# Sums of feed-forward weight quarters: by accumulating loads, or by GpSimd

## The chip, the cores and the metric

The kernel runs on one core of a Trainium2 chip. The metric is the device time of one execution in microseconds (us). Engines are called as the profile calls them: PE (TensorE, matrix products; PEld is its weight load), DVE (VectorE), ACT (ScalarE), POOL (GpSimd), SP (the queue that issues most loads).

## The reference

A small encoder of two layers, 512 tokens of width 1024, everything in 32-bit floats. Each layer is a feed-forward block, a token mixer (attention), attention into 256 memory tokens, and a second feed-forward block, each followed by a layer norm. So there are four feed-forward blocks. This is the part that matters here, with `D_FF` = 2816:

```python
def swiglu(x, w_gate, w_up, w_down):
    return (jax.nn.silu(x @ w_gate) * (x @ w_up)) @ w_down
...
        y = swiglu(x, ffn_w_gate[i, 0], ffn_w_up[i, 0], ffn_w_down[i, 0])
        x = layer_norm(ALPHA * x + 0.5 * y, ln_g[i, 0], ln_b[i, 0])
```

## The kernel before

**Precision.** Every product is made of three reduced-precision products (`mm3`): an operand is split into a high part, a cast by ACT, and a low part, the residue `source - high` by DVE (`split`, and `wide` for a weight tile of 128x1024). All operands of a product must be split before PE can begin it.

**Seven products for eight.** Inside a feed-forward block, most of the work is done in groups of 512 hidden columns (two ranges of 256, `c1` and `c2`) by a scheme of the Strassen-Winograd kind: a 2 x 2 block product with seven block products, named 1 to 7, in place of eight, at the price of sums of quarters of the operands. `quarters` does this for gate and for up. Its four weight quarters are called here a = (0, c1), c = (0, c2), d = (1, c2), b = (1, c1), where 0 and 1 are the halves of the 1024 input rows. Product 1 uses a, 2 uses b, 4 uses d, 5 uses c + d, 7 uses a + c, 6 uses a + c + d, 3 uses a + b + c + d. `down_steps` does it for the down weights, with quarters 11, 12, 22, 21: t1 = 12 + 11 (product 5), t2 = t1 + 22 (product 6), t3 = 12 + 22 (product 7), and t2 + 21 (product 4).

**How the sums are made before.** Two sums of gate and up (c + d and a + c) and two of down (t1 and t3) are made by DMA: SP loads the first quarter into a tile, and then POOL issues a load of the second quarter into the same tile that adds (`accum_op=ALU.add`). So some quarters are loaded more than once. The other sums (two each) are made by DVE (`mix`).

**Tiles.** Weight quarters, their split parts and hidden activations all live in 27 buffers of 128x1024 floats (tag `slab`), given out in program order. A load can start when its buffer is free. Products go into PSUM banks: three with tag `a` (hidden products), two `d`, three `t`.

**Order.** Every product is a step with three parts, `load`, `prep` (sums and splits) and `product`; `pipeline` calls load three steps and prep one step ahead of the product, and the steps of group g's hidden products alternate with those of the down products of group g - 1. There are four groups after the first in each block (16 in all), and a tail: 256 columns without the scheme, and the last down group, whose results POOL gathers with 128x512 sums into `x` (`gather`). But the instructions aren't issued as they are called: `Graph.record` keeps them, and `Graph.emit` schedules them by a list scheduler with costs in ns from `Graph.cost` and the dependencies of the tiles. Every instruction therefore has line 143 in the profile (`op.call`), and is told by its tiles. Names ending in numbers are single tiles; the profile leaves the numbers out, so the working tiles `t2` and the PSUM banks `t` both read `t` there.

Of the kernel before, what the change touches and what calls it, by code (L numbers as in the profile page):

```python
# [12 lines left out]
F32 = mybir.dt.float32  # L13
# [4 lines left out]
ALU = mybir.AluOpType  # L18
AX = mybir.AxisListType

P = 128
# [42 lines left out]
class Graph:  # L64
# [44 lines left out]
    @staticmethod  # L109
    def cost(engine, method, out, ins, kw):  # L110
        n = 1
        for d in (out if method != "tensor_reduce" else ins[0]).ap[1:]:
            n *= d[1]
        wide = any(z.space == bass.MemoryType.PSUM for z in ins + [out]) if engine != "sync" else False
        if method == "dma_start":
            return max(n * out.ap[0][1] * 4 / 205.0, 600.0) if engine == "sync" else 700.0
        if engine == "tensor":
            return max(n / 2.4 + 14, 111)
        scalars = sum(1 for z in ins if z.ap[-1][1] == 1)
        if engine == "vector":  # L120
            if method == "tensor_scalar" and not wide:
                n = n / 2
            return n / 0.96 + 72 + 60 * scalars + 120 * (method == "scalar_tensor_tensor" and "accum_out" in kw)
        if engine == "scalar":
            return n / 1.2 + (55 if wide else 100) + 45 * scalars + 130 * ("accum_out" in kw)
        if n <= 8:
            return 270.0 if method == "tensor_scalar" else 500.0
        adds = len(ins) == 1 and ins[0].ap[-1][0] != 0 and n == 512
        return n * (0.83 if method == "memset" else 4.2 if adds else 1.85) + 60

    def record(self, engine, method, args, kw):
        kw = dict(kw)
# [120 lines left out]
class Kernel:  # L253
# [276 lines left out]
            ps = self.transposed([(t * P, P, sgs[t][:, b * P : (b + 1) * P]) for t in range(NT)])  # L530
            self.nc.scalar.copy(dst[:, :, b, :], ps.rearrange("p (s n) -> p s n", s=2))

    def load_sum(self, *parts):

        z = self.slab(F32, (P, 4, 256))
        for i, (w, q, c) in enumerate(parts):
            src = w[512 * q : 512 * q + 512, c : c + 256].rearrange("(k p) f -> p k f", p=P)
            if i == 0:
                self.nc.sync.dma_start(out=z, in_=src)
            else:  # L540
                self.nc.gpsimd.dma_start(out=z, in_=src, accum_op=ALU.add)
        return z

    def wide(self, z):
# [1 line left out]
        self.split(z, *got)  # L546
        return got

    def mix(self, dst, x, y, op):
        self.nc.vector.tensor_tensor(out=dst, in0=x, in1=y, op=op)  # L550
        return dst

    def w_halves(self, w, c0):
        return [self.wide(self.load_sum((w, q, c0))) for q in range(2)]

    def hidden(self, wg, wu, c0, dst=None):

# [35 lines left out]
    def quarters(self, w, c1, c2, xs, h, gate, up):  # L593


        nc, mix = self.nc, self.mix
        flat = lambda z: z.rearrange("p b n -> p (b n)")
        raw, left, own = {}, {}, {}
        parts = {
            1: [(w, 0, c1)], 6: [(w, 0, c2), (w, 1, c2)], 2: [(w, 1, c1)], 7: [(w, 0, c1), (w, 0, c2)], 4: [(w, 1, c2)],  # L600
        }
        fill, onto = (1, 6, 5), {2: 1, 7: 6, 4: 6, 3: 5}

        def load(m):
            if m in parts:
                raw[m] = self.load_sum(*parts[m])

        def prep(m):
            if m == 6:
                z = mix(raw[1], raw[6], raw[1], ALU.add)  # L610
            elif m == 3:
                z = mix(raw[2], raw[1], raw[2], ALU.add)
            else:
                z = raw[6 if m == 5 else m]
            left[m] = self.wide(z)

        def done(f, s, z):
            if up:
                if not h:
                    h.extend(self.slab(F32, (P, 2, 2, 256)) for _ in range(2))  # L620
                mix(flat(h[f][:, s]), z, gate[f, s], ALU.mult)
            else:
                y = self.t2(F32) if s == 0 else z
                nc.scalar.activation(y, z, AF.Silu)
                gate[f, s] = y

        def product(m):
            if m in fill:
                own[m] = self.ps("a")
            ps, wt = own[onto.get(m, m)], left.pop(m)  # L630
            for b in range(2):
                for k in range(4):
                    self.mm3(
                        ps[:, b * 256 : b * 256 + 256], [z[:, k, b * P : (b + 1) * P] for z in wt],
                        [z[:, k, :] for z in xs[m]], m in fill and b == 0 and k == 0, k == 3, skip_group_check=True,
                    )
            if m == 1:
                own["c12"], own["c22"] = self.t2(F32), self.t2(F32)
                nc.scalar.copy(own["c12"], ps)
            elif m == 6:  # L640
                mix(ps, ps, own["c12"], ALU.subtract)
                nc.scalar.copy(own["c12"], ps)
            elif m == 5:
                nc.scalar.copy(own["c22"], ps)
            elif m == 7:
                mix(own["c22"], ps, own["c22"], ALU.subtract)
                done(1, 1, own["c22"])
            elif m == 3:
                mix(own["c12"], ps, own["c12"], ALU.subtract)
# [12 lines left out]
    def down_steps(self, h, w, r1, r2, coef, u2, last, fresh=False):  # L662


        nc, mix = self.nc, self.mix
        quarters = {"11": (r1, 0), "12": (r1, 512), "22": (r2, 512), "21": (r2, 0)}
        part = lambda name: w[quarters[name][0] : quarters[name][0] + 256, quarters[name][1] : quarters[name][1] + 512]
        raw, left, right, banks, sums = {}, {}, {}, {}, {}
        flat = lambda z: z.rearrange("p b n -> p (b n)")
        act = lambda i, j: flat(h[j - 1][:, i - 1])  # L670

        def fetch(name, plus=None):

            z = self.slab(F32, (P, 2, 512))
            nc.sync.dma_start(out=z, in_=part(name).rearrange("(b p) f -> p b f", p=P))
            if plus:
                nc.gpsimd.dma_start(out=z, in_=part(plus).rearrange("(b p) f -> p b f", p=P), accum_op=ALU.add)
            return z

        def load(m):  # L680
            if m == 1:
                raw["11"] = fetch("11")
            elif m == 6:
                raw["t1"], raw["22"] = fetch("12", "11"), fetch("22")
            elif m == 2:
                raw["21"] = fetch("21")
            elif m == 7:
                raw["t3"] = fetch("12", "22")

        def prep(m):  # L690
            if m == 6:
                raw["t2"] = mix(self.slab(F32, (P, 2, 512)), raw["t1"], raw["22"], ALU.add)
                sums[1] = mix(self.t2(F32), act(2, 2), act(2, 1), ALU.subtract)
                sums[2] = mix(self.t2(F32), sums[1], act(1, 1), ALU.add)
            elif m == 4:
                mix(raw["21"], raw["t2"], raw["21"], ALU.add)
            elif m == 3:
                sums[4] = mix(self.t2(F32), sums[2], act(1, 2), ALU.subtract)
            elif m == 7:
                sums[3] = mix(self.t2(F32), act(1, 1), act(2, 1), ALU.subtract)  # L700
            right[m] = self.wide(raw[{1: "11", 6: "t2", 2: "21", 5: "t1", 3: "22", 7: "t3", 4: "21"}[m]])
# [57 lines left out]
    def ffn(self, i, ln_i, last, aside=None):  # L759

        nc = self.nc
# [32 lines left out]
        tail, wt, ln, ws = [], {}, {}, []  # L794
        for b in range(2):
            for name, w in (("gate", wg), ("up", wu)):

                def load(name=name, w=w):
                    wt[name] = [self.load_sum((w, q, 2560)) for q in range(2)]
# [12 lines left out]

                steps.append((load if b == 0 else none, prep if b == 0 else none, product))
# [717 lines left out]
```

## Time and profile before

| | |
|---|---|
| median of 3 runs | 2249.34 us (2249.16 to 2257.21) |
| the profiled execution | 2246.8 us, of which the span is 2245.0 us |
| granted clock of PE, mean | 0.985 |
| busy: PE, DVE, ACT, POOL | 96%, 75%, 47%, 18% of the span |
| HBM read, written | 301.06 MB, 4.19 MB |

The page gives the busy time of each engine, in all and in 40 slices, the DMA queues, the costliest groups of instructions with what ended the idle time before them, and the DMA issues. q1 in it holds the loads issued by SP, q0 those issued by POOL. A row of a group reads: line, engine, operation, output<-inputs, shape, count | busy us, mean ns of one | idle us before, with the releaser. A row of the timeline reads: start in us from the span's start, length in us, engine, operation, tiles, count of merged instructions, and in brackets the idle time before it and what ended it.

### The profile page before, as it was taken

To read this page: it belongs to the slowest core of one execution; us is meant where nothing else is said; L and a number is where in the kernel's file an instruction comes from. 1 tells how busy PE (TensorE), PEld (TensorE's weight loads), DVE (VectorE), ACT (ScalarE), POOL (GpSimd) and SP (SyncE) were. 2 spreads that over 40 slices of the span, in tenths; PEclk is the share of its full clock that TensorE was granted. 3 is DMA by queue.
4 is the path that set the end of the run, shared out by engine and by line. 5 is a ranking of instruction groups with operands and counts; after the bars stand their busy time and mean duration, and the time that the engine had idled before them with its cause. 6 is when DMAs were issued, how large, how long until landed. Compare 5 with 4: busy or idle time off the path is not lost. (4 is left out here: it accounts for less than half of the span.)

```text
span 2245.0 us, 34046 instructions
## 1 busy us (share of the span) xinstructions
PE 2158.3 (96%) x13408; PEld 1936.2 (86%) x13408; DVE 1689.0 (75%) x2429; ACT 1064.1 (47%) x1671; POOL 398.1 (18%) x499
## 2 busy tenths in 40 slices
PE   9989998999999999999999999999999999999998
PEld 7979887778898898988789998788989989998886
DVE  7678877788854867977767888876677458687886
ACT  5554443467443544544435554435554435454442
POOL 0111004644100001110211111314330000110102
PEclk9999999999999999999999999999999999999999
DMA  7777662201442348776446777535653324577662
GB/s 225 168 165 189 163 176 76 72 10 49 131 142 93 106 126 222 176 176 181 121 102 165 174 174 178 178 96 140 167 159 118 127 86 121 133 183 173 174 174 75
DMA packets 249808, 317.95 MB, mean 142 GB/s; under 512 B 11824, under 2 KB 193712, under 8 KB 249648
## 3 DMA queue, kind: packets, MB, share of 16 engines
q1 hardware_dynamic: 201040, 248.40, 35.7%
q0 software_dynamic: 48320, 67.12, 17.3%
q8 instruction: 105, 1.72, 0.3%
q14 instruction: 55, 0.45, 0.1%
q10 hardware_dynamic: 288, 0.26, 0.0%
HBM read 301.06 MB, written 4.19 MB: 136 GB/s over the span
## 5 line engine op out<-in xcount | busy, mean ns | idle before, releaser
L143 DVE TENSOR_TENSOR slab<-slab,slab 128x1024 fp32r<-128x1024 f32 (+3 forms) x582 | 660.9, 1160 | 159.0 <-ACT slab L143 87.5
L143 ACT CAST slab<-slab 128x1024 fp32r<-128x1024 f32 (+2 forms) x478 | 455.2, 984 | 317.9 <-DMA slab<-ffn_w_gate 93.8
L143 PE MATMUL a<-slab,slab 128*128 128x256 f32 (+3 forms) x2744 | 595.3, 309 | 2.3 <-DVE slab L143 1.2
L143 PE MATMUL a<-xh,slab 128*128 128x256 f32 (+2 forms) x2480 | 559.8, 315 | 1.2 <-ACT slab L143 1.2
L143 PEld LDWEIGHTS a<-slab,slab 128*128 128x128 f32 x2744 | 452.9, 193 | 34.5 <-DVE slab L143 5.0
L143 PE MATMUL d<-slab,slab 128*128 128x512 f32 (+2 forms) x1856 | 456.2, 384 | 5.9 <-ACT slab L143 3.1
L143 PEld LDWEIGHTS a<-xh,slab 128*128 128x128 f32 x2480 | 417.0, 191 | 34.7 <-ACT slab L143 2.1
L143 PE MATMUL a<-raw,slab 128*128 128x256 f32 x2048 | 402.9, 289 | 38.0 <-DVE t L143 31.7
L143 PE MATMUL a<-xl,slab 128*128 128x256 f32 (+1 forms) x1240 | 390.5, 315 | 0.0
L143 PEld LDWEIGHTS d<-slab,slab 128*128 128x128 f32 x1856 | 330.4, 190 | 63.2 <-ACT slab L143 4.8
L143 PEld LDWEIGHTS a<-raw,slab 128*128 128x128 f32 x2048 | 337.1, 197 | 51.5 <-DVE t L143 39.1
L143 PEld LDWEIGHTS a<-xl,slab 128*128 128x128 f32 x1240 | 236.4, 191 | 17.8
L143 PE MATMUL t<-slab,slab 128*128 128x512 f32 (+1 forms) x792 | 195.3, 386 | 7.7 <-ACT slab L143 4.6
L143 DVE TENSOR_TENSOR slab<-raw,slab 128x1024 fp32r<-128x1024 f32 (+2 forms) x140 | 170.6, 1236 | 13.3 <-ACT slab L143 12.9
L143 PEld LDWEIGHTS t<-slab,slab 128*128 128x128 f32 x792 | 138.6, 191 | 33.2 <-ACT slab L143 5.0
L143 ACT CAST slab<-t 128x512 fp32r<-128x512 f32 (+2 forms) x205 | 109.8, 564 | 120.3 <-PE t L143 66.8
L143 DVE TENSOR_TENSOR slab<-t,slab 128x512 fp32r<-128x512 f32 (+2 forms) x205 | 129.8, 656 | 28.6 <-ACT slab L143 28.4
L143 POOL TENSOR_TENSOR t<-t,l 128x256 f32<-128x256 f32 (+2 forms) x104 | 84.4, 832 | 369.1 <-DVE l L143 368.8
L143 ACT CAST slab<-raw 128x1024 fp32r<-128x1024 f32 (+1 forms) x132 | 131.4, 1026 | 22.9 <-DMA raw<-mem_w_kv 7.9
L143 DVE SCALAR_TENSOR_TENSOR x<-d,x 128x512 f32<-128x512 f32 x164 | 111.5, 685 | 29.4 <-PE d L143 28.8
L143 ACT COPY t<-a 128x512 f32<-128x512 f32 x96 | 56.0, 584 | 155.8 <-PE a L143 81.6
L143 POOL DMA_DIRECT2D slab<-ffn_w_up x32 | 41.0, 1282 | 437.4 <-DVE slab L143 176.9
(124 smaller groups left out, 2273.6 us busy)
## 6 DMA issues: line engine op xcount, KB each, us to landing
slab<-ffn_w_gate SPq DMA_DIRECT2D x102, 512.0 KB
slab<-ffn_w_up SPq DMA_DIRECT2D x102, 512.0 KB
slab<-ffn_w_down SPq DMA_DIRECT2D x100, 512.0 KB
slab<-ffn_w_down POOLq DMA_DIRECT2D x40, 512.0 KB, 8.0
slab<-ffn_w_gate POOLq DMA_DIRECT2D x32, 512.0 KB, 7.7
slab<-ffn_w_up POOLq DMA_DIRECT2D x32, 512.0 KB, 6.3
slab<-t SPq DMA_DIRECT2D x96, 128.0 KB
raw<-mem_w_kv SPq DMA_DIRECT2D x8, 1024.0 KB
```

The source lines that it names most:

```text
L143: op.call = lambda: fn(*args, **kw)
```

## The change

Each quarter is loaded once, by SP, into a tile of its own (`quarter` in place of `load_sum`, and `fetch` without `plus`). The sums that the accumulating loads made are made by POOL: v = a + c into a new tile and c += d in place for gate and up, t1 = 12 + 11 into a new tile and 12 += 22 in place for down (`mix` with `aside`). DVE makes the same number of sums as before: a += c after POOL's c += d (which gives a + c + d), a += b, t2 = t1 + 22, t2 += 21. Load m = 6 now takes c and v, load m = 5 takes d. In the scheduler's costs a POOL sum of 1024 columns is now put at 3.8 ns a column.

```diff
-        adds = len(ins) == 1 and ins[0].ap[-1][0] != 0 and n == 512
-        return n * (0.83 if method == "memset" else 4.2 if adds else 1.85) + 60
+        adds = n == 1024 or len(ins) == 1 and ins[0].ap[-1][0] != 0 and n == 512
+        return n * (0.83 if method == "memset" else 3.8 if adds else 1.85) + 60
...
-    def mix(self, dst, x, y, op):
-        self.nc.vector.tensor_tensor(out=dst, in0=x, in1=y, op=op)
+    def mix(self, dst, x, y, op, aside=False):
+        (self.nc.gpsimd if aside else self.nc.vector).tensor_tensor(out=dst, in0=x, in1=y, op=op)
         return dst
...
-        parts = {
-            1: [(w, 0, c1)], 6: [(w, 0, c2), (w, 1, c2)], 2: [(w, 1, c1)], 7: [(w, 0, c1), (w, 0, c2)], 4: [(w, 1, c2)],
-        }
+        places = {1: ("a", 0, c1), 6: ("c", 0, c2), 5: ("d", 1, c2), 2: ("b", 1, c1)}
...
         def load(m):
-            if m in parts:
-                raw[m] = self.load_sum(*parts[m])
+            if m in places:
+                name, q, c = places[m]
+                raw[name] = self.quarter(w, q, c)
+            if m == 6:
+                raw["v"] = mix(self.slab(F32, (P, 4, 256)), raw["a"], raw["c"], ALU.add, True)
+            elif m == 5:
+                mix(raw["c"], raw["c"], raw["d"], ALU.add, True)
 
         def prep(m):
             if m == 6:
-                z = mix(raw[1], raw[6], raw[1], ALU.add)
+                mix(raw["a"], raw["a"], raw["c"], ALU.add)
             elif m == 3:
-                z = mix(raw[2], raw[1], raw[2], ALU.add)
-            else:
-                z = raw[6 if m == 5 else m]
-            left[m] = self.wide(z)
+                mix(raw["a"], raw["a"], raw["b"], ALU.add)
+            left[m] = self.wide(raw[{1: "a", 6: "a", 5: "c", 2: "b", 7: "v", 4: "d", 3: "a"}[m]])
...
             elif m == 6:
-                raw["t1"], raw["22"] = fetch("12", "11"), fetch("22")
+                fetch("12")
+                fetch("22")
+                raw["t1"] = mix(self.slab(F32, (P, 2, 512)), raw["12"], raw["11"], ALU.add, True)
             elif m == 2:
-                raw["21"] = fetch("21")
-            elif m == 7:
-                raw["t3"] = fetch("12", "22")
+                fetch("21")
+                mix(raw["12"], raw["12"], raw["22"], ALU.add, True)
...
-            elif m == 4:
-                mix(raw["21"], raw["t2"], raw["21"], ALU.add)
+            elif m == 2:
+                mix(raw["t2"], raw["t2"], raw["21"], ALU.add)
```


On POOL, in the first feed-forward block, where the third and fourth groups' weights are handled, before (a DMA is an accumulating load, with the tile it adds into):

```order
L143 DMA slab_318_399<-ffn_w_down 128x2x512
L143 DMA slab_338_419<-ffn_w_gate 128x4x256
L143 DMA slab_355_436<-ffn_w_down 128x2x512
L143 DMA slab_358_439<-ffn_w_gate 128x4x256
L143 DMA slab_384_465<-ffn_w_up 128x4x256
L143 DMA slab_406_487<-ffn_w_up 128x4x256
```

And in the change (slab_334 is a, slab_338 is c, slab_343 is d and slab_339 is v of a gate; slab_357, 340 and 358 are 12, 11 and 22 of a down group):

```order
L143 TENSOR_TENSOR slab_339_420<-slab_334_415,slab_338_419 128x1024
L143 TENSOR_TENSOR slab_338_419<-slab_338_419,slab_343_424 128x1024
L143 TENSOR_TENSOR slab_359_440<-slab_357_438,slab_340_421 128x1024
L143 TENSOR_TENSOR slab_357_438<-slab_357_438,slab_358_439 128x1024
L143 TENSOR_TENSOR slab_386_467<-slab_382_463,slab_385_466 128x1024
L143 TENSOR_TENSOR slab_385_466<-slab_385_466,slab_395_476 128x1024
```

Each accumulating load has become one sum on POOL, and the two sums of one weight now stand next to each other. The same gate on DVE before, where slab_334 is a and slab_338 is the sum of c and d by DMA (TENSOR_SCALAR with a bank d or t empties a down product):

```order
L143 TENSOR_SCALAR x3_7_88<-d_333_414,x3_7_88 128x512
L143 TENSOR_TENSOR slab_334_415<-slab_338_419,slab_334_415 128x1024
L143 TENSOR_TENSOR slab_353_434<-slab_338_419,slab_352_433 128x1024
L143 TENSOR_TENSOR t2_300_381<-a_314_395,t2_300_381 128x512
L143 TENSOR_TENSOR slab_343_424<-slab_334_415,slab_342_423 128x1024
```

And in the change, where DVE's sum into slab_334 and the residue of slab_338 come after POOL's second sum:

```order
L143 TENSOR_TENSOR t2_302_383<-a_317_398,t2_302_383 128x512
L143 TENSOR_TENSOR slab_320_401<-t2_302_383,t2_256_337 128x512
L143 TENSOR_SCALAR x2_6_87<-d_330_411,x2_6_87 128x512
L143 TENSOR_TENSOR slab_334_415<-slab_334_415,slab_338_419 128x1024
L143 TENSOR_SCALAR x3_7_88<-d_333_414,x3_7_88 128x512
L143 TENSOR_TENSOR slab_345_426<-slab_334_415,slab_344_425 128x1024
L143 TENSOR_TENSOR slab_355_436<-slab_338_419,slab_354_435 128x1024
```

DVE's sum has moved behind one more down product, and the sum that empties a bank "a" into t2 is now ahead of it; the instructions are the same in kind and number.

More of the change, by code (lines that the diff above doesn't have):

```diff
@@ L531, in ffn_by_tokens, with quarter @@
             self.nc.scalar.copy(dst[:, :, b, :], ps.rearrange("p (s n) -> p s n", s=2))
-    def load_sum(self, *parts):
+    def quarter(self, w, q, c):
         z = self.slab(F32, (P, 4, 256))
[L536 to L539, printed above, removed]
-            else:
-                self.nc.gpsimd.dma_start(out=z, in_=src, accum_op=ALU.add)
+        self.nc.sync.dma_start(out=z, in_=w[512 * q : 512 * q + 512, c : c + 256].rearrange("(k p) f -> p k f", p=P))
         return z
@@ L547, in wide @@
         return got
-    def mix(self, dst, x, y, op):
-        self.nc.vector.tensor_tensor(out=dst, in0=x, in1=y, op=op)
+    def mix(self, dst, x, y, op, aside=False):
+        (self.nc.gpsimd if aside else self.nc.vector).tensor_tensor(out=dst, in0=x, in1=y, op=op)
         return dst
     def w_halves(self, w, c0):
-        return [self.wide(self.load_sum((w, q, c0))) for q in range(2)]
+        return [self.wide(self.quarter(w, q, c0)) for q in range(2)]
     def hidden(self, wg, wu, c0, dst=None):
@@ L598, in quarters @@
         raw, left, own = {}, {}, {}
-        parts = {
-            1: [(w, 0, c1)], 6: [(w, 0, c2), (w, 1, c2)], 2: [(w, 1, c1)], 7: [(w, 0, c1), (w, 0, c2)], 4: [(w, 1, c2)],
-        }
         fill, onto = (1, 6, 5), {2: 1, 7: 6, 4: 6, 3: 5}
+        places = {1: ("a", 0, c1), 6: ("c", 0, c2), 5: ("d", 1, c2), 2: ("b", 1, c1)}
         def load(m):
-            if m in parts:
-                raw[m] = self.load_sum(*parts[m])
+            if m in places:
[5 more added lines that the diff above has]
+                mix(raw["c"], raw["c"], raw["d"], ALU.add, True)
         def prep(m):
             if m == 6:
-                z = mix(raw[1], raw[6], raw[1], ALU.add)
+                mix(raw["a"], raw["a"], raw["c"], ALU.add)
             elif m == 3:
-                z = mix(raw[2], raw[1], raw[2], ALU.add)
-            else:
-                z = raw[6 if m == 5 else m]
-            left[m] = self.wide(z)
+                mix(raw["a"], raw["a"], raw["b"], ALU.add)
+            left[m] = self.wide(raw[{1: "a", 6: "a", 5: "c", 2: "b", 7: "v", 4: "d", 3: "a"}[m]])
         def done(f, s, z):
@@ L670, in down_steps, with fetch @@
         act = lambda i, j: flat(h[j - 1][:, i - 1])
-        def fetch(name, plus=None):
-            z = self.slab(F32, (P, 2, 512))
+        def fetch(name):
+            z = raw[name] = self.slab(F32, (P, 2, 512))
             nc.sync.dma_start(out=z, in_=part(name).rearrange("(b p) f -> p b f", p=P))
-            if plus:
-                nc.gpsimd.dma_start(out=z, in_=part(plus).rearrange("(b p) f -> p b f", p=P), accum_op=ALU.add)
-            return z
         def load(m):
             if m == 1:
-                raw["11"] = fetch("11")
+                fetch("11")
             elif m == 6:
-                raw["t1"], raw["22"] = fetch("12", "11"), fetch("22")
+                fetch("12")
+                fetch("22")
+                raw["t1"] = mix(self.slab(F32, (P, 2, 512)), raw["12"], raw["11"], ALU.add, True)
             elif m == 2:
-                raw["21"] = fetch("21")
-            elif m == 7:
-                raw["t3"] = fetch("12", "22")
+                fetch("21")
+                mix(raw["12"], raw["12"], raw["22"], ALU.add, True)
         def prep(m):
@@ L700, in prep @@
                 sums[3] = mix(self.t2(F32), act(1, 1), act(2, 1), ALU.subtract)
-            right[m] = self.wide(raw[{1: "11", 6: "t2", 2: "21", 5: "t1", 3: "22", 7: "t3", 4: "21"}[m]])
+            right[m] = self.wide(raw[{1: "11", 6: "t2", 2: "21", 5: "t1", 3: "22", 7: "12", 4: "t2"}[m]])
             z = {1: lambda: act(1, 1), 2: lambda: act(1, 2), 4: lambda: act(2, 2)}.get(m) or (lambda: sums[{6: 2, 5: 1, 7: 3, 3: 4}[m]])
@@ L798, in load @@
                 def load(name=name, w=w):
-                    wt[name] = [self.load_sum((w, q, 2560)) for q in range(2)]
+                    wt[name] = [self.quarter(w, q, 2560) for q in range(2)]
                 def prep(name=name):
```

## The prediction

> **What bounds the kernel now.** I read the page's first view, then its groups, then stretches of 60 us inside the feed-forward blocks, then who is waited for. The first view says that TensorE (PE) is the bound and that VectorE (DVE) is next.
>
> ```profile
> PE 2158.3 (96%) x13408; PEld 1936.2 (86%) x13408; DVE 1689.0 (75%) x2429; ACT 1064.1 (47%) x1671; POOL 398.1 (18%) x499
> ```
>
> PE is idle for 2245.0 - 2158.3 = 87 us, which is all that any change beside PE's own work can win. The change touches the feed-forward blocks, so the share of DVE has to be read there. The view by stretches was asked for twelve stretches of 60 us in the middle of the four blocks; one row of it, and its sum:
>
> ```profile
> 880.00:940.00 60.00, 58.74 (x406) 54.09 (x405) 52.75 (x62) 29.90 (x38) 7.61 (x7) 1.00 0.83 203
> 940.00:1000.00 60.00, 54.85 (x370) 50.74 (x370) 47.08 (x57) 29.18 (x36) 7.53 (x6) 0.97 0.64 155
> 1330.00:1390.00 60.00, 57.74 (x394) 53.59 (x393) 49.95 (x60) 28.91 (x36) 7.55 (x6) 0.97 0.74 177
> sum 720.00, PE 691.87 PEld 642.54 DVE 596.94 ACT 349.17 POOL 83.39; mean PE 57.66 PEld 53.54 DVE 49.75 ACT 29.10 POOL 6.95
> ```
>
> The columns are the length, then busy time and instructions of PE, weight loads, DVE, ACT and POOL, then clock and DMA. In 60 us, PE works 57.7 us and DVE 49.75 us: DVE has some 10 us to spare, and PE waits 2.3 us. POOL's six or seven instructions are the accumulating loads of one group of columns (two for gate, two for up, two for down), so such a stretch is about one group; there are 4 x 4 = 16 groups. What PE waits for, in windows that hold the four blocks:
>
> ```profile
> PE a L143 <- DVE t L143: 6.8, 3, 4.5
> PE a L143 <- DVE t L143: 9.1, 3, 4.0
> PE a L143 <- DVE t L143: 5.6, 4, 2.2
> PE a L143 <- DVE t L143: 10.3, 5, 4.2
> ```
>
> 31.8 us, always for a PSUM bank "a" that DVE has not emptied. One of these stalls, from the timeline:
>
> ```profile
> 292.78 1.05 ACT L143 CAST slab<-slab 128x1024 fp32r<-128x1024 f32 x1 [2.18 <-DMA slab<-ffn_w_down]
> 300.81 0.68 DVE L143 TENSOR_TENSOR t<-a,t 128x512 f32<-128x512 f32 x1
> 301.54 0.58 PE L143 MATMUL a<-raw,slab 128*128 128x256 f32 x1 [4.55 <-DVE t L143]
> ```
>
> A late load of down weights holds ACT, ACT's casts hold DVE's residues, and the sum that frees the bank stands behind them in DVE's queue. So DVE's queue is the near-bound of these blocks; DMA enters only through it.
>
> **The change part by part.** *Removed: 104 accumulating loads and 52 plain ones.*
>
> ```profile
> slab<-ffn_w_down POOLq DMA_DIRECT2D x40, 512.0 KB, 8.0
> slab<-ffn_w_gate POOLq DMA_DIRECT2D x32, 512.0 KB, 7.7
> slab<-ffn_w_up POOLq DMA_DIRECT2D x32, 512.0 KB, 6.3
> q1 hardware_dynamic: 201040, 248.40, 35.7%
> q0 software_dynamic: 48320, 67.12, 17.3%
> L143 DVE TENSOR_TENSOR slab<-slab,slab 128x1024 f32<-128x1024 f32 x104 | 126.6, 1221 | 70.8 <-DMA slab<-ffn_w_up 31.9 <-DMA slab<-ffn_w_down 25.3 <-DMA slab<-ffn_w_gate 13.1
> ```
>
> All of those 104 go, and one plain load for each gate or up call of quarters (32) and each down group (20). That is 156 x 0.524 = 82 of the two queues' 316 MB. Traffic bounds nothing here for long, so the saving counts only where a load is late: DVE sat 70.8 us before its 104 sums, mostly for loads of 6 to 8 us that could start only after another load. Of PE's 31.8 us I credit a small part, 4 us, because the long stalls begin with a plain load of down weights, which stays, behind less traffic. SP's queue is 52 issues shorter and keeps its order otherwise.
>
> *Added: 104 sums of 128x1024 on POOL.* No such row exists. The nearest are POOL's sums of two SBUF operands with 256 and 512 columns, from the views of the tiles slab and x (least, median and longest time):
>
> ```profile
> L143 POOL TENSOR_TENSOR slab<-t,t x20: 729/740/2368, 395.0 to 494.9; 128x256 f32<-128x256 f32 x16, 128x512 f32<-128x512 f32 x4
> L143 POOL TENSOR_TENSOR x<-x,slab x24: 1280/1728/2281, 340.9 to 2217.6; 128x512 f32<-128x512 f32 x24
> ```
>
> Undisturbed, 256 columns cost 0.74 us and 512 cost 1.28, so 1024 should cost 1.28 + 2 x 0.54 = 2.36 us (an estimate). POOL has room for 104 x 2.36 = 245 us. What matters is what DVE does meanwhile. The timeline of the gathers at the end of the third block shows it:
>
> ```profile
> 1459.92 1.28 POOL L143 TENSOR_TENSOR x<-x,slab 128x512 f32<-128x512 f32 x1
> 1459.94 1.81 DVE L143 TENSOR_TENSOR slab<-slab,slab 128x512 fp32r<-128x512 f32 x1
> 1461.67 0.68 DVE L143 SCALAR_TENSOR_TENSOR x<-t,x 128x512 f32<-128x512 f32 x1
> 1462.84 2.28 POOL L143 TENSOR_TENSOR x<-x,slab 128x512 f32<-128x512 f32 x1
> ```
>
> A DVE sum of two SBUF tiles that starts 0.02 us after POOL's takes 1.81 us where 0.68 is usual: it lost 1.13 of POOL's 1.28 us. The DVE instruction that reads PSUM and one SBUF tile is not slowed, and POOL's own sum grows to 2.28 us when DVE was first. So one of the two stands still while the other runs. [...]
>
> How often is DVE's next instruction of the blocked kind? From the groups by form between 880 and 1060 us, and the row of that stretch:
>
> ```profile
> L143 DVE TENSOR_TENSOR slab<-slab,slab 128x1024 fp32r<-128x1024 f32 x62 | 74.6, 1219 | 14.7 <-ACT slab L143 14.6
> L143 DVE TENSOR_TENSOR slab<-slab,slab 128x1024 f32<-128x1024 f32 x16 | 19.4, 1221 | 9.1 <-DMA slab<-ffn_w_up 6.2 <-DMA slab<-ffn_w_down 2.8
> L143 DVE TENSOR_TENSOR slab<-t,slab 128x512 fp32r<-128x512 f32 x9 | 6.1, 683 | 0.0
> L143 DVE TENSOR_TENSOR slab<-slab,slab 128x512 fp32r<-128x512 f32 x8 | 5.5, 684 | 0.0
> 880.00:1060.00 180.00, 148.63 (x175) 0.98 0.72 177
> ```
>
> 95 in these four rows, 113 of 175 with the small groups, have two SBUF inputs: 0.65. POOL gets its turn when such an instruction ends. With a chance of 0.65 the next one is blocked for the whole 2.36 us; with 0.35 a PSUM instruction of 0.68 us runs first, and so on: 0.65 x 2.36 + 0.35 x 0.65 x 1.68 + 0.35 x 0.35 x 0.65 x 1.00 + ... = 2.0 us. DVE is busy 148.63 / 180 = 0.83 of the time, so 1.7 us is lost per sum. The bounds are 0 (DVE idle or on PSUM) and 2.36.
>
> *The sum for a group:* 49.75 + 6 x 1.7 = 60 us of DVE in a stretch of 60, in which PE needs 57.7. DVE becomes the bound. It cannot be full: the fullest row above has 52.75 of 60 (0.88) while PE was the bound; I take 0.95 for a DVE that is itself the bound (a choice between 0.88 and 1). 60 / 0.95 = 63.1, so +3.1 us, x 16 groups = +50 us. With every sum blocking in full, the upper bound: (49.75 + 14.2) / 0.95 = 67.3, +117 us.
>
> *The rest.* The other 8 sums (two for down at the end of each block) cost 8 x 1.7 = 14 us of DVE where fewer products need it: +4. DVE's own sums keep their number. New waits: 52 of DVE's sums (a += c after POOL's c += d, and t2 after t1) now wait for POOL, and what queues behind them on DVE are PSUM evacuations, for which PE waits. POOL's sums need only plain loads, where DVE before waited for a load after a load, so I cost this at nothing (with POOL's pair of sums late, up to 1.5 us each). Tiles: v and d are taken three steps earlier, about one more of 27 buffers; hidden by the shorter loads. Sum: +50 + 4 - 4 = **+50 us**. The profiled execution took 2246.8 us (2245.0 span and 1.8 around it), the median of the runs 2249.3, so 2.5 higher: 2246.8 + 50 + 2.5 = **2299 us**.
>
> **The rivals.** *Faster: the late loads go and the sums hide (0.15).* The point is the loss per sum: PE needs 57.66 and DVE 49.75, so up to (57.66 - 49.75) / 6 = 1.3 us the sums fit beside PE. If POOL's sums fall into the 70.8 us in which DVE sat waiting for sums of loads, the loss is below that, and with 82 MB less two thirds of the 31.8 us of stalls go: 2249 - 20 = 2229 us. Against it: 0.65 of DVE's instructions are blocked, and POOL's sum is ready just when DVE has work.
>
> *They fit and nothing is won (0.15):* about 2249 us, a loss near 1.3 us per sum with the old stalls.
>
> *Long stalls halve the clock (0.14).* After a stall of 1.54 us a pair of matmuls takes 0.40 us, after one of 3.97 us it takes 0.63:
>
> ```profile
> 954.42 0.39 PE L143 MATMUL a<-raw,slab 128*128 128x256 f32 x1 [1.54 <-DVE t L143]
> 954.76 0.40 PE L143 MATMUL a<-raw,slab 128*128 128x256 f32 x2
> ...
> 1053.54 0.39 PE L143 MATMUL a<-raw,slab 128*128 128x256 f32 x1 [3.97 <-DVE t L143]
> 1054.36 0.63 PE L143 MATMUL a<-raw,slab 128*128 128x256 f32 x2
> ...
> 1057.53 0.40 PE L143 MATMUL a<-raw,slab 128*128 128x256 f32 x2
> ```
>
> The slow spell lasts some 3.4 us, until 1057.5. If the new loss comes in lumps of 4 us, each brings some 3.4 us at about half speed, 1.7 us lost; one or two more such spells per group, 27 to 54 us on top: about 2345 us. [...]
>
> *POOL is late (0.06):* if the 52 waits cost 1 to 1.5 us each as well, +52 to 78: about 2365 us.
>
> **How the numbers follow.** My forecast has 0.50, with its own range of 2262 to 2335 (loss per sum 1.4 to 2.1). About 0.5% is what a measurement of this kernel can tell from no change, 11 us. Slower holds the forecast, the clock and the late POOL: 0.70. Same is 0.15, faster 0.15. The range leaves out most of the faster case and a little above the late POOL: 2238 to 2365.
>
> **What would show it.** Right: POOL rows of 128x1024 near 2.4 us at least and 3 us or more in the median; DVE's residues "slab<-slab,slab 128x1024" rising from 1219 to a mean of 1.5 us or more; DVE busy 0.93 or more in the 60 us stretches; PE's waits for DVE in the four blocks up from 32 to 80 us; q0 down to 13 MB and q1 to 221. Wrong: DVE rows that stay at 1.22 us while POOL adds; or PE's waits below 25 us with DVE slowed all the same, since then its spare time took everything.

## The result, and the profile after

The change is a little faster, not slower: the median of 5 runs is 2237.4 us against 2249.9, a ratio of 0.9932 with a 95% interval of 0.9912 to 0.9953. The profiled execution took 2237.4 us (span 2235.6). The forecast, 2299 with a range of 2238 to 2365, missed on the side of its first rival (2229).

The first view, the two queues, the costliest rows that are new, and the residues, all of the change:

```profile
PE 2153.6 (96%) x13408; PEld 1924.2 (86%) x13408; DVE 1821.6 (81%) x2429; ACT 1060.4 (47%) x1671; POOL 556.4 (25%) x499
q1 hardware_dynamic: 178704, 221.14, 32.2%
q0 software_dynamic: 3648, 12.59, 1.9%
L143 POOL TENSOR_TENSOR slab<-slab,slab 128x1024 f32<-128x1024 f32 x104 | 295.1, 2838 | 883.2 <-PE t L143 345.8 <-DMA slab<-ffn_w_down 167.3 <-PE a L143 100.2
L143 DVE TENSOR_TENSOR slab<-slab,slab 128x1024 fp32r<-128x1024 f32 x408 | 571.4, 1428 | 23.1 <-ACT slab L143 22.3
L143 DVE TENSOR_TENSOR slab<-slab,slab 128x1024 f32<-128x1024 f32 x104 | 125.6, 1216 | 0.0
```

The residues before:

```profile
L143 DVE TENSOR_TENSOR slab<-slab,slab 128x1024 fp32r<-128x1024 f32 x408 | 493.4, 1227 | 84.9 <-ACT slab L143 84.1
```

Much is as forecast: the queues moved 221 and 13 MB, a POOL sum takes 2.84 us in the mean, DVE's residues went from 1.23 to 1.43 us, and DVE, which made the same instructions as before, was busy 1821.6 - 1689.0 = 132.6 us longer: 1.28 us per POOL sum. That a DVE instruction with two SBUF inputs and a POOL sum hold each other up, called the lock from here on, can be read off the timeline (DVE, then POOL):

```profile
1293.87 6.66 DVE L143 TENSOR_TENSOR slab<-slab,slab 128x1024 fp32r<-128x1024 f32 x3 [0.57 <-ACT slab L143]
1301.07 0.68 DVE L143 TENSOR_TENSOR a<-a,t 128x512 f32<-128x512 f32 x1
...
1292.06 2.92 POOL L143 TENSOR_TENSOR slab<-slab,slab 128x1024 f32<-128x1024 f32 x1 [7.14 <-DMA slab<-ffn_w_down]
1295.06 3.26 POOL L143 TENSOR_TENSOR slab<-slab,slab 128x1024 f32<-128x1024 f32 x1
```

Three residues take 6.66 us beside two POOL sums, where three in a row beside no POOL sum take 3.49 to 3.50 us in the kernel before; the sum into bank "a" stands behind them. And yet the kernel is faster. What went away is waiting for loads. ACT's waits for feed-forward loads before (us in total, times, longest):

```profile
ACT slab L143 <- DMA slab<-ffn_w_gate: 93.8, 25, 10.2
ACT slab L143 <- DMA slab<-ffn_w_up: 56.4, 32, 3.6
ACT slab L143 <- DMA slab<-ffn_w_down: 51.4, 27, 6.7
```

The same rows in the change:

```profile
ACT slab L143 <- DMA slab<-ffn_w_gate: 20.6, 5, 5.3
ACT slab L143 <- DMA slab<-ffn_w_up: 19.6, 11, 2.9
ACT slab L143 <- DMA slab<-ffn_w_down: 0.5, 1, 0.5
```

201.6 us became 40.7, and the 70.8 us that DVE sat before its own 104 sums became 0 in the change (the last of the rows of the change above). So two large effects seemed to stand against each other. The experiments separate them.

### The profile page after: what moved, and what is told of

Read it like the earlier page. It is cut to its first block, busy times and chain, and to the rows that moved or that the text cites. A ratio compares the mean times of both kernels' runs of the same rounds, so it can differ in the third digit from the quotient of the medians.

```text
span 2235.6 us, 33852 instructions
## 1 busy us (share of the span) xinstructions
PE 2153.6 (96%) x13408; PEld 1924.2 (86%) x13408; DVE 1821.6 (81%) x2429; ACT 1060.4 (47%) x1671; POOL 556.4 (25%) x499
## 4 chain that ended last, share of the span: by engine, by line
PE 67%; DVE 25%; issue 3%; ACT 2%; POOL 1%; DMA 0%; DVEq 0%; SPq 0%; POOLq 0%; ACTq 0%
PE a L143 41%; DVE slab L143 19%; PE d L143 17%; PE t L143 10%; DVE t L143 3%; DVE x L143 2%; ACT slab L143 1%; POOL slab L143 1%; DVE a L143 0%; POOL rms8y L143 0%; ACT t L143 0%; DMA gain<-ab_k_gain 0%; ACT junk L143 0%; POOL lny L143 0%; DMA raw<-x_t 0%
## 5 line engine op out<-in xcount | busy, mean ns | idle before, releaser
L143 DVE TENSOR_TENSOR slab<-slab,slab 128x1024 fp32r<-128x1024 f32 (+3 forms) x582 | 756.3, 1336 | 23.1 <-ACT slab L143 22.3
L143 PE MATMUL a<-slab,slab 128*128 128x256 f32 (+3 forms) x2744 | 589.2, 307 | 2.2 <-ACT t L143 1.1
L143 POOL TENSOR_TENSOR slab<-slab,slab 128x1024 f32<-128x1024 f32 x104 | 295.1, 2838 | 883.2 <-PE t L143 345.8
L143 PEld LDWEIGHTS a<-slab,slab 128*128 128x128 f32 x2744 | 448.0, 191 | 34.2 <-DVE slab L143 5.0
L143 PE MATMUL a<-raw,slab 128*128 128x256 f32 x2048 | 398.2, 287 | 38.7 <-DVE t L143 17.5
L143 PEld LDWEIGHTS a<-raw,slab 128*128 128x128 f32 x2048 | 331.2, 193 | 59.1 <-DVE slab L143 21.2
L143 ACT CAST slab<-t 128x512 fp32r<-128x512 f32 (+2 forms) x205 | 110.1, 563 | 90.0 <-PE t L143 67.5
```

The costliest lines, as they stand in the source:

```text
L143: op.call = lambda: fn(*args, **kw)
```

## The experiments

The expectations of the first runs set two theories against each other: A, the lock costs about what the relief of the loads wins; B, POOL's sums hide and cost nothing (what each means for a run stands in its expectation). Later ones ask what in POOL's sums costs time: the lock itself, the latency of the sums, the order that the scheduler makes, DVE's total time, or the grain (single standstills that make DVE empty a bank late, whatever its total).

The runs were made on several chips, where the kernel before had medians of 2247.4 to 2250.1 us, so 3 us between two of them say nothing. And a run whose sums were placed anew by the scheduler has another order of instructions; the order alone moved the change itself between 2230 and 2250 us (under "Telling the scheduler").

**Without the lock.** First, 8 columns are summed and the others filled with zeros by a memset:

```diff
+        if aside:
...
+            self.nc.gpsimd.tensor_tensor(out=dst[:, :, 0:8], in0=x[:, :, 0:8], in1=y[:, :, 0:8], op=op)
+            self.nc.gpsimd.memset(dst[:, :, 8:n], 0.0)
...
```

> The change, but POOL adds only 8 of each 1024 columns and fills the rest with zeros (a memset reads no SBUF), so the sums are left out and the loads are as in the change. Theory A (the lock on DVE costs what the relief of the loads wins): DVE's residues go back to 1.22 us, DVE busy falls from 1822 to near 1690 us, and the time falls below the change's 2237 by 10 to 25 us, to 2212 to 2227. Theory B (POOL's sums hide in DVE's spare time and cost nothing; the 12 us are all that the loads can give): DVE busy falls as well, the time stays within 5 us of 2237.

Measured: 2172.3 us, ratio 0.9659 (0.9634 to 0.9683), DVE 1694.5 us. A had the sign and far too small a size. This kernel's schedule differs from the change's, so two more were run in which the stand-in is put in only when the instruction is issued, after scheduling; the rows of PE, DVE, ACT and SP stand in the change's order:

```diff
+        if engine == "gpsimd" and method == "tensor_tensor" and op.ns > 2500:
+            op.call = lambda: self.stand_in(**kw)   # 8 columns, then the memset three times (or once)
...
```

> The change with every instruction of PE, DVE, ACT and SP in the same order, but where POOL's sum stood it adds 8 columns and then fills the other columns with zeros three times over (sums left out), some 3 us of POOL in all, as long as the sum took (2.84 us), but reading nearly no SBUF. Lock theory (DVE standing still beside POOL costs the 65 us between 2237 and 2172): about 2172, up to 2185. Latency theory (what waits for the sums waits too long): about 2237. Order theory (the scheduler, told 3.95 us a sum, put the rest in a bad order): about 2237.

> As the run before, in the same order, but the zeros are filled in once, some 1.2 us of POOL. Lock theory: about 2172, as the long one. Latency theory: 2172 to 2185, well under the long one. Order theory: about 2237.

Measured: 2172.8 us, ratio 0.966 (0.9621 to 0.97), and 2174.0, ratio 0.9664 (0.9631 to 0.9697). The same order, with a POOL that is as long at work (598.7 us in the long one, 556.4 in the change) but sums only 8 columns in 1024, is 64.6 us faster than the change. The latency and the order theory fall. These kernels leave the sums out, so part of what PE multiplies is zeros; that isn't what makes them fast, since the run below with all sums on DVE has the same time. DVE in the long one:

```profile
PE 2131.7 (98%) x13408; PEld 1919.9 (88%) x13408; DVE 1691.4 (78%) x2429; ACT 1063.9 (49%) x1671; POOL 598.7 (28%) x811
```

So everything in the change but POOL's sums is worth 2250 - 2173 = 77 us (the relief of the loads, as "Which loads" shows for most of it), and POOL's sums give 64.6 of them back.

**The lock without the relief.** The kernel before, with 104 POOL sums to the junk tile beside its own work:

```diff
+    def idle_sum(self, z):
+        flat = z.rearrange("p b n -> p (b n)")
+        self.nc.gpsimd.tensor_tensor(out=self.junk, in0=flat, in1=flat, op=ALU.add)
...
```

> The kernel before with all its accumulating loads, and beside them 104 POOL sums of 128x1024 whose result goes to the junk tile. Theory A: DVE loses some 1.3 us per sum (busy 1689 to about 1820 us) with no relief of the loads, so the time rises by 15 to 50 us, to 2265 to 2300. Theory B: DVE busy rises as well but the time stays within 10 us of 2250.

Measured: 2259.4 us, ratio 1.0045 (1.0025 to 1.0066); DVE 1794.1 us. Below A's range, and within theory B's 10 us of 2250. The lock is there, though a little smaller (105 us of DVE's time where the change's sums took 133), and the kernel pays 9 us for it, not 65. So the two effects do not simply add: where loads already hold the blocks up, most of the lock seems to fall into time that is lost anyway.

**The sums on DVE.** One line of the change, `mix` without `aside`:

```diff
-        (self.nc.gpsimd if aside else self.nc.vector).tensor_tensor(out=dst, in0=x, in1=y, op=op)
+        self.nc.vector.tensor_tensor(out=dst, in0=x, in1=y, op=op)
```

> The change with its 104 sums on DVE instead of POOL. Each costs DVE some 1.14 to 1.22 us (119 to 127 us in all), where POOL's cost it 1.28 us by the lock (133 us in all). Theory A: DVE busy is about 1810 to 1820, the same as with POOL, and the time is within 12 us of 2237: giving the sums to POOL takes nothing off DVE. Theory B (POOL takes real work off DVE): 20 us or more slower than 2237.

Measured: 2172.9 us, ratio 0.9661 (0.9637 to 0.9686). Both theories fall: DVE's time is 1799.1 us, somewhat under A's 1810 to 1820, and the kernel is 64.5 us faster than the change. It computes the whole reference, and is the fastest such kernel of the study. The sums in it are 104 of these 208 rows:

```profile
L143 DVE TENSOR_TENSOR slab<-slab,slab 128x1024 f32<-128x1024 f32 x208 | 252.6, 1217 | 14.5 <-DMA slab<-ffn_w_down 12.2 <-DMA slab<-ffn_w_up 1.9
```

A sum's row is 1.22 us long, but DVE's instructions overlap a little (their rows add up to 1952.0 us in this run, its busy time is 1799.1), so that DVE's busy time rose by only 1799.1 - 1689.0 = 110.1 us, 1.06 us a sum, when DVE makes them; it rose by 1.28 us a sum when POOL does. Nothing is taken off DVE. Could the 22.5 us more of DVE time explain 64 us of the kernel's? To see, DVE's time was raised without a lock:

```diff
...
+        if aside:
+            z = x[:, 0, 0:192]
+            self.nc.vector.tensor_tensor(out=self.junk[:, :192], in0=z, in1=z, op=op)
```

> The 104 sums on DVE, and behind each a further DVE sum of 192 columns (modelled 0.27 us, result to the junk tile), 28 us in all, so that DVE's time per group rises from 56.5 to about 58.1 us, what it was in the change, without any lock. Total theory: the groups stretch from 59.6 towards 64 us, 2215 or more. Grain theory: 2173 to 2188.

Measured: 2175.9 us, ratio 0.9676 (0.9649 to 0.9703). Its first view, and a stretch of 180 us inside a block:

```profile
PE 2134.2 (98%) x13408; PEld 1921.1 (88%) x13408; DVE 1823.1 (84%) x2637; ACT 1062.3 (49%) x1671; POOL 263.9 (12%) x395
...
1165.00:1345.00 180.00, 180.00 (x1266) 168.98 (x1266) 177.44 (x219) 87.39 (x112) 3.38 (x4) 1.00 0.36 107
```

The stretches that hold the same block, before and in the change:

```profile
1210.00:1390.00 180.00, 175.88 (x1222) 163.98 (x1221) 151.71 (x179) 89.53 (x112) 21.36 (x17) 0.99 0.73 176
...
1200.00:1380.00 180.00, 171.19 (x1176) 157.32 (x1175) 168.17 (x176) 82.63 (x105) 48.49 (x17) 0.99 0.34 103
```

The same DVE time as in the change (1823 and 1822 us), and 61 us less. In the stretch DVE is busy 177.44 of 180 us and PE loses nothing: 1266 products, where the change has 1176 with DVE at 168.17, and the long stand-in above 1270 with DVE at 160.03. The total theory falls.

**What the lock does beyond its time.** In the change's order, each POOL sum is issued in four pieces:

```diff
...
+        for i in range(4):
+            part = lambda z: flat(z)[:, 256 * i : 256 * i + 256]
+            self.nc.gpsimd.tensor_tensor(out=part(out), in0=part(in0), in1=part(in1), op=op)
```

> The change in its own order of instructions, with every POOL sum issued as four sums of 256 columns (0.74 us each undisturbed, 2.96 us a sum instead of 2.36). Total theory (the loss is DVE's total time, which the lock raises past what fits beside PE): DVE loses as much or more, 2235 to 2280. Grain theory (the loss comes from single standstills of 2.2 us, often two in a row, that make DVE empty a PSUM bank late; DVE's total does not matter): DVE gets a turn every 0.74 us and the time falls to 2215 or less.

Measured: 2204.4 us, ratio 0.9804 (0.9776 to 0.9833), 33 us faster than the change, as the grain theory had it. But DVE's total fell too, to 1781.8 us, so the grain is not shown to be what counts. Next, the lost time without a lock: the short stand-in of above, and in its place in the order also a DVE sum of 1024 columns that the scheduler does not know of.

```diff
...
+        self.nc.vector.tensor_tensor(out=junk, in0=flat(xh), in1=flat(xl), op=op)
```

> The change in its own order, without the lock (8 columns summed and the rest filled with zeros on POOL), and at the place of each POOL sum an extra DVE sum of 1024 columns of the activations (1.22 us, result to the junk tile) that the scheduler does not know of: as much DVE time as the lock took (1.28 us a sum), at nearly the same places, but taken in DVE's own order. If the loss is that DVE's order was not planned for the lost time, 2215 to 2240. If it lies in the lock itself (standstills of 2.2 us at places that the order cannot choose), 2173 to 2195.

Measured: 2195.5 us, ratio 0.9776 (0.9748 to 0.9804); DVE 1800.8 us. Just above the lock's range and well under the other: 108 us of DVE time that the scheduler did not know of (1800.8 against 1692.5 in the short stand-in) cost 22 us, where planned time (the run with more DVE work) costs 3 and the lock's 129 us cost 65. So unplanned time of this kind accounts for about a third of the loss. The rest goes with the lock itself: standstills that fall wherever POOL starts, of up to 2.4 us (the longest residue in the change takes 3.62 us, one beside no POOL sum 1.22).

**One sum of the two.** The early sums (c + d, 12 + 11) or the late ones (a + c, 12 + 22) alone on POOL, the others on DVE:

```diff
-                raw["v"] = mix(self.slab(F32, (P, 4, 256)), raw["a"], raw["c"], ALU.add, True)
+                raw["v"] = mix(self.slab(F32, (P, 4, 256)), raw["a"], raw["c"], ALU.add)   # e15; e11 the others
```

> The sums that are needed first (c + d, 12 + 11) on DVE, the late ones (a + c, 12 + 22) on POOL: 52 locks, none behind another. Total theory: half of the loss, about 2205. Grain theory: single blocks without pairs, 2178 to 2195.

> The first sums on POOL, the late ones on DVE: 52 locks, the complement of the run with the late ones on POOL (2214). If the loss of 65 us belongs to the locks one by one, the two losses add up to it: 41 us there, so about 24 here, near 2197. If a sum that is needed soon costs more on POOL, 2215 or more here.

Measured: late ones on POOL 2213.7 us, ratio 0.9843 (0.9815 to 0.9871); early ones 2207.5, ratio 0.9827 (0.9799 to 0.9855). Both lie above the figures that were set for them (2205 at most; 2197, if the losses add). That is 41 and 35 us over 2173, 76 together where both cost 65: locks cost without being in pairs, and an early sum is not seen to be dearer than a late one. The guess that pairs were to blame falls.

**Telling the scheduler.** The change with other costs, 2.25 ns a column, or 2.7 and DVE held 1.3 us per POOL sum:

```diff
...
+            if op.held:
+                now["vector"] = max(now["vector"], t) + 1300.0
```

> The change with whole sums on POOL and a modelled cost of 2.25 ns a column (2.36 us) in place of 3.8, which reorders some of DVE. Lock and latency theory: 2225 to 2245, nothing to win. Order theory: 2200 or less.

> The change with whole sums on POOL, the scheduler told 2.7 ns a column and that each such sum holds DVE for 1.3 us. Lock theory: the blocks still fall where they fall, 2215 to 2240. Order theory, in the form that an order that leaves room on DVE hides the lock: 2200 or less.

Measured: 2229.9 us, ratio 0.9911 (0.9876 to 0.9946), and 2250.4, ratio 1.0 (0.998 to 1.0019). The first is within the range of the lock theory; the second is slower than its range. Neither order hides the lock, and by themselves the orders differ by 20 us.

**Which loads.** Where do the 77 us come from? First the bytes: the sums on DVE, and 156 copies of quarters from HBM to HBM:

```diff
...
+        self.nc.after = self.nc.ops[-1], {"gpsimd"}
+        copy = self.tile(self.dram, list(z.shape), F32, "spare", 8)
+        self.nc.gpsimd.dma_start(out=copy, in_=src)
```

> The 104 sums on DVE, and 156 copies of weight quarters from HBM to HBM, issued by POOL when a quarter has landed: the 82 MB that the change took away are read again (and written), but nothing waits for them. Traffic theory (the relief was that fewer bytes share the DMA engines): 2200 or more. Chain theory (the relief was that no sum waits any more for a load that may only start after another load): 2170 to 2185.

Measured: 2176.5 us, ratio 0.9678 (0.9645 to 0.971), with as many bytes read as before:

```profile
HBM read 301.06 MB, written 85.98 MB: 178 GB/s over the span
```

As many bytes from HBM cost 4 us. (The copies land in HBM and not in SBUF.) So the bytes were not the cost. Then the accumulating loads themselves, half of them at a time: the late sums by DMA with the early ones on POOL, the early ones by DMA with the late ones on DVE (which load c and 12 once more), and the late ones by DMA with the early ones on DVE.

```diff
+                raw["v"] = self.load_sum((w, 0, c1), (w, 0, c2))   # e4, e14; e13: load_sum for c + d
```

> The change, but the two sums that are needed last (a + c of gate and up, 12 + 22 of down) are made by accumulating loads again; POOL makes only c + d and 12 + 11. Theory A: half the lock (DVE busy about 1755 us) and two thirds of the relief for the urgent sums: 2220 to 2237, as fast as the change or faster. Theory B: the loads are what matters, so with half the accumulating loads back half the gain is lost: 2240 to 2246.

> The sums needed first (c + d, 12 + 11) by accumulating loads as in the kernel before, the late ones (a + c, 12 + 22) on DVE; no POOL sums. Chain theory (what the change relieved is the wait for a load that starts only after another has landed, where its sum is needed soon): most of the 77 us come back, 2220 to 2250. Any accumulating load costs alike: half, about 2210. Rival (neither matters without the other): 2173 to 2190.

> The late sums by accumulating loads, the first ones on DVE; no POOL sums. Chain theory: the late sums have time to land, 2170 to 2185. Any accumulating load costs alike: about 2210.

Measured: 2199.6 us, ratio 0.978 (0.9754 to 0.9806); 2191.2, ratio 0.9756 (0.9722 to 0.979); 2215.7, ratio 0.9867 (0.9838 to 0.9896). The first is faster than both of its theories allowed. The second lies just above its rival's range, far from the chain theory's, and the third where any accumulating load was to cost alike. So accumulating loads cost, 18 us for the early sums and 43 for the late ones, 61 of the 77; but the expectation that the early sums would be the dear ones was the wrong way round. In the last of the three, ACT waits for the quarters of gate, and PE for ACT:

```profile
ACT slab L143 <- DMA slab<-ffn_w_gate: 70.5, 21, 7.4
...
PE a L143 <- ACT slab L143: 13.1, 11, 3.5
```

Of the 70.5 us, 57.2 were ended by an accumulating load. A "late" sum of gate or up by DMA is only asked for when its own buffer is free, then takes two loads one after the other, and so is not there in time. That reading fits the waits; it was not tested by itself. Nor do ACT's waits alone give the price: with the early sums by DMA they are longer (133.7 us for the three feed-forward weights against 100.9), and that run is 24 us faster. What tells the two apart is PE's waits for "a" on DVE's "t", DVE's "slab" and ACT's "slab": 5.7 us with the early sums by DMA, 30.0 with the late ones. And the first of the three, with both 52 locks and 52 accumulating loads, loses 27 us, less than the 35 and 43 of its two halves: these losses do not add either.

## Why the prediction was wrong

*The lock: right.* That one of the two stands still while the other runs was read from the gathers, and the trace of the change shows it: of 408 residues the 89 that run beside a POOL sum for more than 0.3 us take 2.19 us in the median, the others 1.22, while of 164 sums `x<-d,x`, which read a PSUM bank, the 35 that run beside one take 0.69 us at most, as the others do. The estimate of 2.36 us for a POOL sum stands against a least duration of 2.38, and what lies above it (2.84 us in the mean) is put down to waiting for DVE: the 44 sums that start beside no DVE sum of two SBUF tiles take 2.41 us in the median, the other 60 take 3.09. The loss per sum was put at 1.7 us and measured 1.28, just under the 1.3 us that the first rival named as the point from which it decides.

*DVE's fill: wrong in kind.* "It cannot be full: I take 0.95" was the step that turned DVE time into kernel time. The run with more DVE work shows DVE at 177.44 of 180 us with PE at full rate, so DVE's total does not limit at 0.95 or at 0.98. The +50 us of this step came close to the measured 64.6 by luck: against the short stand-in, 129 us of DVE time cost 65 us by the lock, 108 unplanned ones 22, and 131 planned ones (1692.5 to 1823.1) 3. The total that the step reckons with is not what decides.

*The relief of the loads: mis-sized, and this turned the sign.* It was credited 4 us; it is 77. The reason given was "the long stalls begin with a plain load of down weights, which stays". That was misread. The row of ACT's wait until 292.78 names `ffn_w_down`, which both queues load, and the semaphore that ended this wait is one that only POOL's loads raise. On POOL's own timeline (of before) stand the loads that ended this wait and the one before it, until 288.61:

```profile
281.62 1.28 POOL L143 DMA_DIRECT2D slab<-ffn_w_up  x1 [14.98 <-DVE slab L143]
283.02 1.19 POOL L143 DMA_DIRECT2D slab<-ffn_w_down  x1
```

Both are accumulating loads, just what the change takes away; the second landed at 292.76. The stalls of 3.97 us (until 1053.54) and 4.23 us (until 2170.45) have two such loads behind them as well. Told apart in this way, accumulating loads ended 162.6 of the 201.6 us that ACT waited for feed-forward weights, and practically all that DVE waited for them. PE's waits over the whole span, longest first, before:

```profile
PE a L143 <- DVE t L143: 31.7, 15, 4.5
PE t L143 <- DVE x L143: 14.6, 8, 7.5
PE a L143 <- DVE slab L143: 5.5, 11, 1.5
...
PE a L143 <- ACT slab L143: 3.1, 2, 1.9
```

In the change:

```profile
PE a L143 <- DVE t L143: 17.5, 17, 1.2
PE a L143 <- DVE slab L143: 16.9, 27, 4.4
PE t L143 <- DVE x L143: 10.8, 6, 5.2
PE a L143 <- ACT slab L143: 8.1, 5, 3.1
```

With the sums on DVE:

```profile
PE 2131.6 (98%) x13408; PEld 1919.9 (88%) x13408; DVE 1799.1 (83%) x2533; ACT 1062.7 (49%) x1671; POOL 260.5 (12%) x395
...
PE t L143 <- DVE x L143: 11.3, 7, 5.2
...
PE a L143 <- ACT slab L143: 1.1, 1, 1.1
...
PE a L143 <- DVE slab L143: 1.0, 5, 0.3
...
PE a L143 <- DVE t L143: 0.2, 1, 0.2
```

The row that the prediction took as its bound, 31.7 us for "a" from DVE's "t", does not shrink by 4: it shrinks to 0.2. All three rows for "a" together fall from 40.3 to 2.3 us, and PE's whole idle time from 2245.0 - 2158.3 = 86.7 us to 2169.5 - 2131.6 = 37.9. The step that failed has two parts: the load that was to stay is one that goes, and PE's busy time was taken as fixed. It fell by 26.7 us for the same 13408 products, with the mean granted clock up from 0.985 to 0.994. 48.8 us of idle time and 26.7 of busy time are the 75.5 us by which the two spans differ. The slow spell after a stall, which the prediction used for a rival only, is a good part of the busy time: the traces hold 13 spells at half clock (70 us) before, 7 (40 us) in the change and 3 (27 us) with the sums on DVE. In them a product of 256 columns follows the last after 213 ns in place of 120, and by the 182 and 44 products that fall into them they cost some 20 us before and 5 with the sums on DVE (an estimate). Where the other 12 of the 26.7 us lie is open.

In the change the stalls for "a" come back as 49 mostly shorter ones, 42.5 us in these three rows, where the long stand-in, in the same order without the lock, has 2.4: that is the lock seen from PE.

*Where the sign turned.* The trace can also be read by place: PE's order is nearly the same in these three kernels, so one can ask how long each takes for the products of the prediction's twelve stretches. Before, they took 720 us; in the change 728; with the sums on DVE 677. There, in the middle of the blocks, the change is indeed slower, as forecast: the lock costs 51 us and the relief, 43, doesn't quite pay for it. In the rest of the kernel the lock costs 15 us and the relief is 33, and the change wins 18. The prediction read DVE's load where the lock weighs most and credited the relief, there and elsewhere, next to nothing.

*"Traffic bounds nothing here":* right, and shown by the copies. *DVE's waits for its sums (70.8 us):* they went, as said, but were priced only through the same 4 us: that was part of the same miss. *The new waits for POOL,* priced at nothing, were next to nothing: those 104 sums have no idle time before them, and ACT waited once, 2.9 us, for a tile of POOL's. *The clock rival* went the other way: the mean granted clock rose from 0.985 to 0.992 in the change, whose new stalls are mostly of a length that no slow spell followed in the traces (the longest for DVE's "t" is 1.2 us, and no single stall of 1.54 us or less was followed by one). *The rivals:* the first named the mechanism that won, but still with the sums hidden; its time, 2229, is 8 us off by luck. The sums did not hide: 77 us won, 65 lost.

*The signs.* POOL's rows (2.38 us at least, 2.73 in the median) and the residues (1.43 us) came near to what was named, DVE was busy 56.92 of 60 us in twelve stretches (0.95), and the queues fell as said. PE's waits for DVE's "t" in the four blocks fell from 31.8 to 17.5 us where 80 were forecast. That is a sign named for "wrong", but not for its reason, that DVE's spare time took everything: the lock costs 65 us, and the waits for DVE's "slab" rose from 5.5 to 16.9 us.

What stays open: why a standstill by the lock costs 0.50 us of the kernel per us of DVE time (65 for 129) and unplanned DVE time 0.20 (22 for 108), whether by its length or by its places. Smaller pieces halve the loss, but they also shorten the total. Also open is what in an accumulating load costs the time, and which part of the 16 us of relief that neither half shows is due to the two together.

## What to carry to other kernels

An elementwise sum of two SBUF tiles moved from VectorE to GpSimd took nothing off a VectorE that mostly works on two SBUF tiles: it lost 1.28 us per sum to save 1.06, at times that its order could not choose. Before a late load is said to stay, look for its issue: two queues loaded the same weights here, and a row that names the weights doesn't say which. Before a step is costed by its engine's total, ask whether the same work in a planned place costs anything at all; here DVE at 98% (177.44 of 180 us) cost 3 us. And compare the time for the same products, stage by stage and at the ends of the blocks too: here the change lost in the middle of the blocks what it more than won around it.

## What the runs showed of the hardware

Equal DVE time is not equal: 104 sums of 1024 columns and 104 of 192 in DVE's own order cost 3 us (131 us of its busy time), and 129 us of standstill beside POOL cost 65. Raising the HBM traffic to a mean of 178 GB/s (301 MB read, 86 MB written) cost 4 us. In the three traces (before, the change, the sums on DVE) every stall of 2.2 us or more of a PE at full clock was followed by a spell at half clock or ended in one; the spells last 3.41, 6.83 or 10.24 us in the first two, but for the one at the end of each. Single stalls of 1.54 us or less were not, and of the four single ones of about 1.8 us three were (until 411.13 and 1452.03 before, and until 402.10 in the change). The two stalls that the prediction shows, of 1.54 us (clock 1.00 from 954.4 to 957.8) and 3.97 us (0.50 from 1054.1 to 1057.5), lie far apart, and a single stall far shorter than the longer one can be enough: after the one of 2.24 us that ended at 1349.75 in the kernel before, the clock was 0.50 from 1351.1 to 1354.4. A POOL memset of 992 columns, 0.93 us, did not slow DVE: its residues, 1227 ns before, stayed at 1232 in the run with three of them per sum:

```profile
L143 DVE TENSOR_TENSOR slab<-slab,slab 128x1024 fp32r<-128x1024 f32 x408 | 490.9, 1232 | 33.4 <-ACT slab L143 32.5
L173 POOL MEMSET slab<- 128x992 f32 x192 | 178.1, 928 | 7.4
```
